# Token tiles of the output projection in another order, its moving operands split in parts, and finer rings for the product by w_out

## The chip, the cores and the metric

The kernel runs on one core of a Trainium2 chip. The metric is the time of one execution on the device in microseconds (us), as a median of runs; lower is better. Beside the runs there is one execution that the hardware profiler recorded, and all rows of the profile come from it. The engines are named as in the profile: PE is TensorE (matmuls, with PEld its weight loads), DVE is VectorE, ACT is ScalarE, POOL is GpSimd, and SP is the engine that issues the DMA transfers here. L12 is line 12 of the kernel before.

## The reference

The kernel computes a trunk of two encoder layers over 1024 tokens of width 1024, all in float32:

```python
for i in range(DEPTH):                      # 2 layers
    g = norm_g[i]
    h = rms_norm(x, g[0])
    if i % 2 == 0:
        m = neighborhood_attention(h, ...)  # 16 heads, 8 x 16 windows on a 16 x 64 grid
    else:
        m = diff_attention(h, ...)          # 8 heads, dense, T5 bias
    # both mixers end with  o @ w_o  (1024 x 1024), the output projection
    x = x + rms_norm(m, g[1])
    f = conv_glu_ffn(rms_norm(x, g[2]), w_in, conv_w, conv_b, w_out)
    x = x + rms_norm(f, g[3])
    gate = jax.nn.sigmoid(rms_norm(x, g[4]) @ ple_w_gate[i])
    x = x + gate * (p[i] @ ple_w_proj[i])

def conv_glu_ffn(h, w_in, conv_w, conv_b, w_out):
    gate, val = split(h @ w_in, 2)          # w_in 1024 x 5632, halves of 2816
    gate = conv3(gate, conv_w) + conv_b     # along the tokens, per channel
    return (gelu_tanh(gate) * val) @ w_out  # w_out 2816 x 1024
```

## The kernel before, in words

**Matmuls and splits.** A product of two float32 matrices is made of three matmuls on split operands (`mm3`, L107 to L109, and `times_steps`, L635): each operand is cut into a high part, rounded by ACT (L85), and a low part, which DVE makes as the operand minus the high part (L86). A split (`split`, L81) is therefore one ACT and one DVE instruction, the second waiting for the first. A matmul takes a stationary block of 128 x 128 and a moving block of 128 x 512. Transposes (L137) are matmuls with an identity matrix, eight for a token tile of 128 tokens.

**Order.** Only PE's order is the order of the program text (`manual_schedule`). DVE, ACT, POOL and the SP queue are ordered by a planner, which runs the program through a timeline of its own, takes what is ready and prefers what stands earlier in the text. Each engine then works strictly in that order. Tiles come from pools with a fixed number of buffers per tag; a tile in a new pool waits for the tiles of the old pool that lay at the same addresses, in the order in which the tags were first asked for.

**The output projection (`mix_out`, L660).** It runs over eight token tiles t. For each, PE makes 48 matmuls with w_o (tile 0 has most of its own earlier). Then follows a chain of one column and one row operation after another: squares on ACT with sums (L734), the sums added on DVE (L735), scaled and EPS added (L120), the power -1/2 on POOL (L121), the normed product on DVE (L739), the residual added (L742), its store, squares again (L115), L120, L121, and the normed h on DVE (L129). The transposes of tile t - 1 stand behind the matmuls of tile t, and `put` (L693) turns their result into the moving operands of the product by w_in. That product is made by Winograd's form of Strassen's method, with seven products of half size for each block of 128 channels: its moving operands are the quadrants B11, B21, B22 and the sums T1 to T4, with B11 and B21 from tiles 0 to 3, and the others needing tile t and tile t - 4 (t from 4 to 7). For t of 4 to 7 `put` makes T1 and T2 on DVE and ACT (L705 to L711) and leaves in b12 and b21, by three sums on POOL (L714, L716), what becomes T3 and T4. After the last tile, T3, B22 and T4 are split whole, 2048 columns each (L752 to L754).

**Begun blocks (`gate_begun`, L785).** After the last tile's matmuls and the transposes of the last tile but one, PE makes two products each on B11 and B21 for the blocks f = 0 and 1 (48 matmuls), while the last tile's h is made; then the last transposes; then `gated` (L801) goes on with the product on T2. The weights' sums S for Strassen's method (L847 to L850) are made on POOL, in the first half of a spare tile; the second half holds p1 of f = 0 and 1 and later Z, the sums of the activations (L900 to L903), which go to memory as the spills S1 to S4, beside the spills A11, A12 and A22.

**The product by w_out (`mixed`, L910).** Seven products (A11, A12, S1, S4, S2, S3, A22), again Strassen's, of 11 K tiles each; a K tile is 12 matmuls. They run in chunks of two K tiles (the last has one): a spill is loaded and split as stationary blocks, a quadrant of w_out, or a difference of two that `over` makes in place on DVE (L950), is split as the moving operand. The splits go to two rings of two slots, a slot holding a chunk. The quadrants lie in six pages of 16 KB per partition, four from the pool r2, two from r1, as rings are; one of these lies under the spare tile and can be loaded when the last spill of Z has been read.

**After it (`embed`, L986).** `residual` (L997) normalises tile t of the result and adds x1; `turn` (L1007) transposes it; then come the gate's matmuls (L635, `g`). `embed` runs the product by w_out as a generator: it takes it up to the sums of S3, emits residual 0 and 1, and goes through A22, with tile 0 turned after the fourth of eleven K tiles. The other tiles are turned ahead of their gate matmuls.

## Time and profile before

| what | value |
|---|---|
| runs | 2834.53, 2834.66, 2828.19 us; median 2834.53 |
| profiled execution, own time | 2829.02 us |
| its span in the profile | 2827.2 us, 36045 instructions |
| mean granted clock of PE | 0.985 of full speed |
| PE busy | 2715.1 us (96%), 13312 matmuls |
| DVE, ACT, POOL busy | 1961.5, 1320.9, 559.1 us |
| output projection, tiles 1 to 7, layers 0 and 1 | from 490.0 to 575.5 us, and to 2051.7 us |
| product by w_in | from there to about 1024 and 2498 us |
| product by w_out | to 1250.5 us in layer 0 |

Rows of a timeline give start, length, engine, line, operation, output and inputs with their shape, and in brackets how long the engine stood idle before it and what released it. Rows of waits give who waited for whom, and then us in total, times, and the longest. Rows of groups end with the count, the busy time, the mean in ns, and the idle time before them. The letter before an arrow is the written tile, by the program's names without their numbers: r stands for pages of both pools r1 and r2, b for a bank of PSUM.

### The profile page before, as it was taken

Reading aid. Unit: us, or ns where it says so; the run is one execution under the profiler, and the core shown is the slowest. Engines: PE = TensorE matmul, PEld = TensorE weight load, DVE = VectorE, ACT = ScalarE, POOL = GpSimd, SP = SyncE. Lnnn points to the kernel's source line nnn. Section 1 sums busy time; section 2 is a strip of 40 time slices with the busy share of each in tenths; the row PEclk is TensorE's granted clock in tenths of the full one; section 3 lists DMA queues with packets and bytes.
Section 4 is the critical chain, followed back from the end, with each engine's and each line's share of the span. In section 5 each row is a group of like instructions: output and inputs, shape, how many; then the busy total and the mean of one; then the engine's idle time right before and its main releaser. Section 6 shows DMA issues by size and latency. Waiting matters only on the chain.

```text
span 2827.2 us, 36045 instructions
## 1 busy us (share of the span) xinstructions
PE 2715.1 (96%) x13312; PEld 2261.6 (80%) x13312; DVE 1961.5 (69%) x3223; ACT 1320.9 (47%) x2331; POOL 559.1 (20%) x513
## 2 busy tenths in 40 slices
PE   7999999979999999999999999999979999999999
PEld 5788887758888878778888888887858888878777
DVE  5677776678777775566677777776677676666564
ACT  4555556444444434354455555565444444434352
POOL 2121220153433401001000000000254334301000
PEclk9999999989999999999999999999989999999999
DMA  6512215512232272243211111115313323372343
GB/s 186 160 52 66 66 45 184 146 58 105 107 109 99 99 287 89 86 155 110 96 45 45 45 45 45 37 52 180 126 60 105 112 98 107 109 261 93 104 147 104
DMA packets 129185, 298.44 MB, mean 106 GB/s; under 512 B 11721, under 2 KB 37705, under 8 KB 129009
## 3 DMA queue, kind: packets, MB, share of 16 engines
q1 hardware_dynamic: 129008, 296.15, 31.7%
q8 instruction: 104, 1.70, 0.2%
q14 instruction: 73, 0.59, 0.1%
HBM read 221.69 MB, written 86.61 MB: 109 GB/s over the span
## 4 chain that ended last, share of the span: by engine, by line
PE 84%; DVE 6%; DMA 5%; issue 2%; ACT 1%; POOL 1%; SPq 0%; DVEq 0%; ACTq 0%; POOLq 0%
PE b L108 19%; PE b L107 19%; PE b L109 19%; PE g L635 6%; PE b L554 4%; PE m L635 4%; DVE r L86 2%; PE s L516 2%; PE s L517 2%; PE b L540 2%; PE b L137 2%; DMA r<-in_ffn_w_out 2%; PE av L427 2%; PE b L411 1%; DMA x<-in_x 1%
## 5 line engine op out<-in xcount | busy, mean ns | idle before, releaser
L107 PE MATMUL b<-r,ws 128*128 128x512 f32 (+1 forms) x1312 | 542.2, 413 | 3.5 <-ACT ws L85 3.5
L109 PE MATMUL b<-r,ws 128*128 128x512 f32 (+1 forms) x1312 | 514.1, 392 | 0.5 <-DVE ws L86 0.5
L108 PE MATMUL b<-r,ws 128*128 128x512 f32 (+1 forms) x1312 | 513.1, 391 | 1.3 <-DVE r L86 1.1
L107 PE MATMUL b<-r,wa 128*128 128x512 f32 x704 | 276.5, 393 | 29.6 <-ACT wa L85 27.8
L121 POOL TENSOR_TENSOR ss<-ss,mhalf 128x1 f32<-128x1 f32 x136 | 86.9, 640 | 1098.1 <-DVE ss L120 1095.7
L109 PEld LDWEIGHTS b<-r,ws 128*128 128x128 f32 x1312 | 249.1, 190 | 53.5 <-DVE ws L86 1.0
L369 ACT ACTIVATE E<-E,mn 128x1024 f32<-128x1024 f32 (+2 forms) x256 | 221.6, 866 | 147.6 <-DVE mn L365 147.0
L107 PEld LDWEIGHTS b<-r,ws 128*128 128x128 f32 x1312 | 250.2, 191 | 48.5 <-ACT ws L85 4.0
L108 PE MATMUL b<-r,r 128*128 128x512 f32 x680 | 268.9, 395 | 14.8 <-DVE r L86 14.8
L108 PEld LDWEIGHTS b<-r,ws 128*128 128x128 f32 x1312 | 250.8, 191 | 38.4 <-DVE r L86 2.6
L109 PE MATMUL b<-r,wa 128*128 128x512 f32 x704 | 275.9, 392 | 4.0 <-DVE wa L86 4.0
L107 PE MATMUL b<-r,r 128*128 128x512 f32 x680 | 270.1, 397 | 6.6 <-ACT r L85 6.2
L108 PE MATMUL b<-r,wa 128*128 128x512 f32 x704 | 275.6, 392 | 0.0
L109 PE MATMUL b<-r,r 128*128 128x512 f32 x680 | 266.8, 392 | 0.0
L85 ACT ACTIVATE r<-raw 128x1024 fp32r<-128x1024 f32 x108 | 108.2, 1003 | 242.6 <-PE b L108 211.8
L86 DVE TENSOR_TENSOR r<-raw,r 128x1024 fp32r<-128x1024 f32 x108 | 126.6, 1173 | 123.5 <-ACT r L85 123.3
L86 DVE TENSOR_TENSOR ws<-raw,ws 128x512 fp32r<-128x512 f32 (+3 forms) x168 | 156.5, 939 | 73.7 <-ACT ws L85 72.0
L85 ACT ACTIVATE ws<-raw 128x512 fp32r<-128x512 f32 (+3 forms) x168 | 124.2, 748 | 145.4 <-PE b L109 57.0
L635 PE MATMUL g<-r,ws 128*128 128x512 f32 x768 | 181.3, 396 | 6.3 <-DVE facc L983 6.3
L107 PEld LDWEIGHTS b<-r,wa 128*128 128x128 f32 x704 | 133.4, 189 | 58.5 <-ACT wa L85 28.2
L365 DVE CUSTOM_DVE_ANT_0 E<-s,T 128x1024 f32<-128x1024 f32 x128 | 156.5, 1223 | 33.8 <-PE s L517 32.8
L635 PEld LDWEIGHTS g<-r,ws 128*128 128x128 f32 x768 | 145.3, 191 | 36.6 <-DVE facc L983 6.8
(173 smaller groups left out, 5360.8 us busy)
## 6 DMA issues: line engine op xcount, KB each, us to landing
raw<-in_w_in SPq DMA_DIRECT2D x88, 512.0 KB, 3.5
raw<-in_qkv SPq DMA_DIRECT2D x48, 512.0 KB, 5.6
spillS<-r SPq DMA_DIRECT2D x88, 256.0 KB, 2.7
r<-in_ffn_w_out SPq DMA_DIRECT2D x40, 512.0 KB, 10.0
raw<-spillS SPq DMA_DIRECT2D x40, 512.0 KB, 3.6
spillA<-cv SPq DMA_DIRECT2D x66, 256.0 KB, 2.6
raw<-spillA SPq DMA_DIRECT2D x30, 512.0 KB, 3.9
x<-x SPq DMA_DIRECT2D x24, 512.0 KB, 3.7
```

What stands on the lines that cost most here:

```text
L85: nc.scalar.activation(hi, src, AF.Copy)
L86: nc.vector.tensor_tensor(out=lo, in0=src, in1=hi.bitcast(F32), op=ALU.subtract)
L107: mm(out, sta[0], mov[0], start=first, stop=False, skip_group_check=onto)
L108: mm(out, sta[0], mov[1], start=False, stop=False, skip_group_check=onto)
L109: mm(out, sta[1], mov[0], start=False, stop=last, skip_group_check=onto)
L121: nc.gpsimd.tensor_tensor(out=ss, in0=ss, in1=self.mhalf, op=ALU.pow)
L137: self.nc.tensor.transpose(t[:, k * P : k * P + P], h[:, c : c + P], self.ident)
L365: nc.vector.tensor_tensor_reduce(out=e, in0=s, in1=bias, scale=1.0, scalar=3e38, op0=ALU.add, op1=ALU.min, accum_out=mn)
L369: nc.scalar.activation(e, e, AF.Exp, bias=mn, scale=-1.0, accum_out=sm)
L427: nc.tensor.matmul(out, V[:, kb, m], a[:, at * P : (at + w) * P], start=i + z == 0, stop=i == len(steps) - 1 and z == 1)
L554: nc.tensor.matmul(o, wT[:, k], V[:, k], start=k == 0, stop=k == KT - 1)
L635: mm(out[half], a, b[:, w], start=first and k + z == 0, stop=last and k == n - 1 and z == 2)
```

## The change

The diff does four things.

1. *The projection.* The tiles are taken in the order 0, 4, 1, 5, 2, 3, 6, 7. The pages of x, then g1 and g2, then h are asked for before b12, b21 and b22. The three sums of `put` for tiles 4 to 7 go from POOL to DVE. `gate_begun` becomes a generator: its first part, the load and the splits of the weights of f = 0, stands before the last tile's matmuls, the rest where all of it stood. The late splits are cut in two: the columns of the first three of their four tiles, for T3, B22 and T4, and after these the columns of the last tile.
2. *Weights' sums.* For f = 0 and 1 the four sums S are made on DVE, for later f on POOL as before.
3. *The product by w_out.* The rings hold four slots of one K tile each, in the same space; each K tile is split by itself (512 columns for 1024). The sixth page is the first half of the spare tile. The difference that S3 takes is made during S2, and the one that A22 takes during S3. The generator gives way before S3, so that residual 0 and 1 stand ahead of S3, and then once a chunk; tiles 0 and 1 are turned after the third and fifth of A22's six chunks.
4. *Columns.* The squares are scaled by 1/32 on ACT; in the projection the two half sums and EPS are added by one instruction with two scalars.

```diff
@@ rstd, rstd_of @@
-        nc.scalar.activation(junk, src, AF.Square, scale=scale, accum_out=ss)
-        nc.vector.tensor_scalar(out=ss, in0=ss, scalar1=1.0 / width, scalar2=EPS, op0=ALU.mult, op1=ALU.add)
+        self.nc.scalar.activation(junk, src, AF.Square, scale=D**-0.5, accum_out=ss)
+        self.nc.vector.tensor_single_scalar(out=ss, in_=ss, scalar=EPS, op=ALU.add)
...
@@ mix_out @@
+            W, last = self.W, self.opage
+            order = (0, 4, 1, 5, 2, 3, 6, 7)
+            ready = [self.page(x, "x"), self.page(x, "x")]
             g1 = self.bcast(x, "g1", self.i["norm_g"][layer, 1], bufs=1)
             g2 = self.bcast(x, "g2", self.i["norm_g"][layer, 2], bufs=1)
+            hs = [self.page(x, "h"), self.page(x, "h")]
             b12, b21, b22 = (self.page(x, k, (P, 4, 512), bufs=1) for k in ("B12", "B21", "B22"))
...
-                        on = nc.gpsimd.tensor_tensor
-                        on(out=of(b21, t), in0=of(b21, t), in1=of(b12, t), op=sub)
+                        tt(out=of(b21, t), in0=of(b21, t), in1=of(b12, t), op=sub)
                         for a in both("B11", t):
-                            on(out=of(b12, t), in0=of(b12, t), in1=a.bitcast(F32), op=sub)
+                            tt(out=of(b12, t), in0=of(b12, t), in1=a.bitcast(F32), op=sub)
...
-            for t in range(NT):
+            for n, t in enumerate(order):
...
-                nc.vector.tensor_tensor(out=ss[0], in0=ss[0], in1=ss[1], op=ALU.add)
-                r = self.rstd_of(ss[0], D)
+                nc.vector.tensor_scalar(out=r, in0=r, scalar1=ss[1], scalar2=EPS, op0=ALU.add, op1=ALU.add)
+                self.root(r)
...
-                if t > 0:
-                    self.transposed(hs[t - 1], put(t - 1))
-            begin(layer, X)
+                if n > 0:
+                    self.transposed(hs[n - 1], put(order[n - 1]))
+                if n == NT - 2:
+                    begin = begin(layer, X)
+                    next(begin)
+            next(begin)
             self.transposed(hs[-1], put(NT - 1))
-            for k, a in (("T3", b12), ("B22", b22), ("T4", b21)):
+            late = (("T3", b12), ("B22", b22), ("T4", b21))
...
+            for k, a in late:
                 X[k] = self.page(self.r1, "r1", (P, 2, 4, 512), F32R)
-                self.split(a, X[k][:, 0], X[k][:, 1])
+                self.split(first_three(a), first_three(X[k][:, 0]), first_three(X[k][:, 1]))
+            for k, a in late:
+                self.split(of(a, NT - 1), *both(k, NT - 1))
...
@@ gated @@
-                tt = nc.gpsimd.tensor_tensor
+                tt = (nc.gpsimd if f > 1 else nc.vector).tensor_tensor
...
@@ mixed @@
-        rings = [self.page(self.r1, "r1", (P, 2, 2, 2, 512), F32R) for _ in range(2)]
-        pages += [self.page(self.r1, "r1", (P, 2, 4, 512)) for _ in range(2)]
+        rings = [self.page(self.r1, "r1", (P, 4, 2, 512), F32R) for _ in range(2)]
+        pages.append(self.page(self.r1, "r1", (P, 2, 4, 512)))
+        pages.append(self.spare[:, :4].rearrange("p (c q) w -> p c q w", c=1))
...
-                self.split(raw[:, :c], sta[:, 0, :c], sta[:, 1, :c])
-                self.split(mov(n), b[:, 0, :c], b[:, 1, :c])
+                b = mov(n)
                 for i in range(c):
+                    at = self.turns % 4
+                    self.turns += 1
+                    (sh, sl), (bh, bl) = ((r[:, at, 0], r[:, at, 1]) for r in rings)
+                    self.split(raw[:, i], sh, sl)
+                    self.split(b[:, i], bh, bl)
...
+        def beside(n, *a):
+            over(n, *a)
+            return n
...
-        whole(one, "S2", lambda n: over(n, 0, 3, 0), True)
+        whole(one, "S2", lambda n: over(beside(n, 1, 3, 1), 0, 3, 0), True)
...
-        whole(one, "S3", lambda n: over(n, 1, 3, 1), False)
+        yield
+        whole(one, "S3", lambda n: quadrant(beside(n, 2, 2, 0), 1), False)
...
-        yield
-        yield from product(one, "A22", lambda n: over(n, 2, 2, 0), False)
+        yield from product(one, "A22", lambda n: quadrant(n, 2), False)
...
@@ embed @@
         for n, _ in enumerate(product):
-            if n == 3:
-                turn(0)
+            if n in (2, 4):
+                turn(n // 2 - 1)
...
-                if t + 1 < NT:
+                if 1 < t + 1 < NT:
                     turn(t + 1)
```

More of the change, by code (lines that the diff above doesn't have):

```diff
@@ L555, in da_values @@
         os = self.page(x, "os", (P, P))
-        r = self.rstd(o, os, P, scale=r0)
+        r = self.col("ss")
+        nc.scalar.activation(os, o, AF.Square, scale=r0, accum_out=r)
+        nc.vector.tensor_scalar(out=r, in0=r, scalar1=1.0 / P, scalar2=EPS, op0=ALU.mult, op1=ALU.add)
+        self.root(r)
         nc.vector.tensor_scalar(out=os, in0=o, scalar1=r0, scalar2=r, op0=ALU.mult, op1=ALU.mult)
@@ L711, in of_group @@
                         self.split(of(b12, t), *both("T2", t))
-                        on = nc.gpsimd.tensor_tensor
-                        on(out=of(b21, t), in0=of(b21, t), in1=of(b12, t), op=sub)
+                        tt(out=of(b21, t), in0=of(b21, t), in1=of(b12, t), op=sub)
                         for a in both("B11", t):
-                            on(out=of(b12, t), in0=of(b12, t), in1=a.bitcast(F32), op=sub)
+                            tt(out=of(b12, t), in0=of(b12, t), in1=a.bitcast(F32), op=sub)
                 return of_group
-            ready = [load(0), load(1)]
-            hs = []
-            for t in range(NT):
+            ready = [load(t, ready[n]) for n, t in enumerate(order[:2])]
+            for n, t in enumerate(order):
                 hi, lo, xi = ready.pop(0)
                 part = [(hi[:, k], lo[:, k]) for k in range(KT)]
-                h = self.page(x, "h")
+                h = hs[n] if n < 2 else self.page(x, "h")
+                if n >= 2:
+                    hs.append(h)
                 if t == 0:
@@ L733, in mix_out @@
                 for half in range(2):
-                    nc.scalar.activation(h[:, half * 512 : half * 512 + 512], m[half], AF.Square, accum_out=ss[half])
-                nc.vector.tensor_tensor(out=ss[0], in0=ss[0], in1=ss[1], op=ALU.add)
-                r = self.rstd_of(ss[0], D)
+                    w = slice(half * 512, half * 512 + 512)
+                    nc.scalar.activation(h[:, w], m[half], AF.Square, scale=D**-0.5, accum_out=ss[half])
+                r = ss[0]
+                nc.vector.tensor_scalar(out=r, in0=r, scalar1=ss[1], scalar2=EPS, op0=ALU.add, op1=ALU.add)
+                self.root(r)
                 for half in range(2):
@@ L785, in gate_begun @@
     def gate_begun(self, layer, X):
-        A = [self.weights_of(layer, 0), None]
+        A = [self.weights_of(layer, 0)]
         o = [[self.operand(A[0]["A11"]), self.operand(A[0]["A12"])]]
-        A[1] = self.weights_of(layer, 1)
+        yield
+        A.append(self.weights_of(layer, 1))
         o.append([self.operand(A[1]["A11"]), self.operand(A[1]["A12"])])
@@ L799, in gate_begun @@
             self.product(self.begun[f][1], o[f][1], X["B21"], False)
+        yield
     def gated(self, layer, X, spill):
@@ L1001, in residual @@
             h[t] = self.page(x, "h", bufs=2)
-            r = self.rstd(f, h[t], D)
+            r = self.rstd(f, h[t])
             nc.vector.scalar_tensor_tensor(out=f, in0=f, scalar=r, in1=g3, op0=ALU.mult, op1=ALU.mult)
```

35 lines of the change are left out of this document (16 added, 19 removed).

## The prediction, made blind

> **What bounds the kernel now.** I read the page first, then the waits of TensorE, then busy time in 20 us stretches, then the timelines of the engines where those stretches are thin.
>
> ```profile
> span 2827.2 us, 36045 instructions
> PE 2715.1 (96%) x13312; PEld 2261.6 (80%) x13312; DVE 1961.5 (69%) x3223; ACT 1320.9 (47%) x2331; POOL 559.1 (20%) x513
> ```
>
> TensorE (PE) is busy 96% of the span, and the change leaves its instructions as they are. What it can win is PE's idle time (2827.2 - 2715.1 = 112 us) and what a lowered clock costs after idle time. The waits of PE over the span:
>
> ```profile
> PE b L107 <- ACT wa L85: 27.8, 2, 13.9
> PE b L108 <- DVE r L86: 15.9, 19, 1.4
> PE b L137 <- DVE h L129: 13.1, 7, 3.1
> PE g L635 <- DVE facc L983: 6.3, 2, 3.3
> PE b L107 <- ACT r L85: 6.2, 3, 3.3
> ```
>
> The first row's two waits of 13.9 us stand once in each layer, at the end of the output projection; the third row's seven are 1.6, 1.7, 3.1 and 1.5 in layer 0 and 1.8, 3.1 and 0.3 in layer 1, at transposes of the projection. Stretches (length, PE busy and its matmuls, weight loads, DVE, ACT, POOL, granted clock, DMA share, GB/s): first a full one, then the thin ones.
>
> ```profile
> 680.00:700.00 20.00, 20.00 (x90) 16.57 (x89) 17.01 (x24) 8.43 (x13) 7.97 (x5) 1.00 0.33 118
> ...
> 580.00:600.00 20.00, 13.28 (x56) 10.46 (x55) 16.10 (x21) 7.00 (x12) 11.24 (x9) 0.84 0.18 53
> 600.00:620.00 20.00, 9.35 (x28) 6.99 (x29) 13.09 (x11) 11.31 (x14) 7.03 (x5) 0.58 0.16 49
> 1040.00:1060.00 20.00, 15.92 (x63) 12.16 (x62) 16.27 (x17) 5.87 (x7) 0.00 (x0) 0.93 0.87 309
> 1060.00:1080.00 20.00, 20.00 (x81) 16.34 (x80) 7.17 (x6) 7.93 (x10) 0.00 (x0) 0.90 0.20 66
> 2520.00:2540.00 20.00, 16.58 (x65) 13.01 (x64) 11.26 (x12) 6.80 (x9) 0.00 (x0) 0.91 0.55 175
> ```
>
> A full stretch holds 90 matmuls, 20/90 = 0.222 us each; 600-620 holds 28. So the losses sit at the end of the projection (560-620, and from 2040 in layer 1) and where the product by w_out begins (1040-1080, 2500-2540).
>
> **End of the output projection, step by step.** PE in layer 0 (the first row an undisturbed tile), then the two rows of layer 1 that answer the second and fifth:
>
> ```profile
> 514.51 1.03 PE L137 MATMUL b<-ident,h 128*128 128x128 f32 x8
> 564.34 11.17 PE L635 MATMUL m<-r,ws 128*128 128x512 f32 x48
> 578.61 1.36 PE L137 MATMUL b<-ident,h 128*128 128x128 f32 x8 [3.10 <-DVE h L129]
> 593.70 1.07 PE L137 MATMUL b<-ident,h 128*128 128x128 f32 x8 [1.50 <-DVE h L129]
> 608.66 0.80 PE L107 MATMUL b<-r,wa 128*128 128x512 f32 x1 [13.89 <-ACT wa L85]
> 611.88 0.79 PE L109 MATMUL b<-r,wa 128*128 128x512 f32 x1 [1.99 <-DVE wa L86]
> ...
> 2040.50 11.16 PE L635 MATMUL m<-r,ws 128*128 128x512 f32 x48
> 2084.68 0.79 PE L107 MATMUL b<-r,wa 128*128 128x512 f32 x1 [13.88 <-ACT wa L85]
> ```
>
> The last tile's matmuls end at 564.34 + 11.17 = 575.5. Then come the transposes of the last tile but one, 48 matmuls on B11 and B21, the last transposes, and at 608.66 the first matmul on T2: 33.2 us after 575.5, of which 48 x 0.227 = 10.9 and two sets of transposes are work. In layer 1 it is 2084.68 - 2051.7 = 33.0. What holds it, on DVE, POOL and ACT:
>
> ```profile
> 523.01 1.28 DVE L129 SCALAR_TENSOR_TENSOR h<-x,ss,g 128x1024 f32<-128x1024 f32 x1 [0.73 <-POOL ss L121]
> 591.26 2.29 DVE L129 SCALAR_TENSOR_TENSOR h<-x,ss,g 128x1024 f32<-128x1024 f32 x1 [0.44 <-POOL ss L121]
> 594.38 0.69 DVE L705 TENSOR_TENSOR B<-b,r 128x512 f32<-128x512 f32 x1 [0.82 <-PE b L137]
> 598.60 1.22 DVE L86 TENSOR_TENSOR r<-B,r 128x512 fp32r<-128x512 f32 x1 [0.70 <-ACT r L85]
> 599.97 2.58 POOL L716 TENSOR_TENSOR B<-B,r 128x512 f32<-128x512 f32 x2 [0.69 <-DVE r L86]
> 602.58 5.51 ACT L85 ACTIVATE r<-B 128x2048 fp32r<-128x2048 f32 x3 [4.01 <-POOL B L716]
> 604.52 6.70 DVE L86 TENSOR_TENSOR r<-B,r 128x2048 fp32r<-128x2048 f32 x3 [4.70 <-ACT r L85]
> ```
>
> T2 is whole at 598.60 + 1.22 = 599.8, but the operand wa stands behind POOL's last sums (to 602.55) and the three splits of 2048 columns on ACT and DVE (to 608.1 and 611.2).
>
> The change takes that queue apart: three quarters of each late split (1536 columns) no longer need the last tile, the sums go from POOL to DVE, the first sums for the weights too, and the pages of x, g1, g2 and h come first in the pool, so that wa no longer lies over B12 and B21, which the late splits read last.
>
> What I expect of the step: 11.7 us of PE work after the last matmuls (transposes 0.8, products 10.9), then the last tile's h. Its chain took 524.29 - 514.51 = 9.8 us where nothing disturbed it (the h at 523.01, of the matmuls that ended as the transposes at 514.51 began), against 593.55 - 575.5 = 18 at the end. With put(6) on DVE in between I allow 13.0, so 1.3 us of wait. From h to the end of T2 it was 599.8 - 593.55 = 6.3 us; I keep 6.5. T2 starts 13.0 + 6.5 = 19.5 us after the last matmuls. Later waits in f = 0 and 1 were 2.0 and 1.9 in layer 0, 2.0 in layer 1; with DVE fuller I charge 3 and 2. **Gain: 33.2 + 3.9 - 19.5 - 3 = 14.6, and 33.0 + 2.0 - 19.5 - 2 = 13.5 us.** Bounds: from 0, if DVE keeps its order, to 20 a layer, if h and operands are never late.
>
> What DVE is given: L714 and L716 on POOL,
>
> ```profile
> L716 POOL TENSOR_TENSOR B<-B,r 128x512 f32<-128x512 f32 x8 | 11.4, 1428 | 1.5 <-DVE r L86 0.7 <-DVE ss L120 0.7
> L714 POOL TENSOR_TENSOR B<-B,B 128x512 f32<-128x512 f32 x4 | 6.9, 1730 | 5.8 <-DVE B L710 5.8
> L129 DVE SCALAR_TENSOR_TENSOR h<-x,ss,g 128x1024 f32<-128x1024 f32 x8 | 13.3, 1658 | 8.8 <-POOL ss L121 8.8
> ```
>
> 12 sums, and 8 for the weights of f = 0 and 1: 20 x 0.62 (the pitch of the 0.69 us at 594.38 and its neighbours) = 12.4 us a layer. It is given back part: L129 takes 1.28 us with POOL at rest and 1658 ns in the mean here, 8 x 0.38 = 3.0 us, and other DVE rows beside POOL's sums are as much longer (the 1.22 at 598.60 for 0.69). I take DVE as 5 to 9 us fuller, which is in the 13.0 and the 3 above. The two other tiles with sums, 4 and 5, now come at steps 1 and 3, where PE has 11.2 us of matmuls over DVE; before, L129 was late by 1.74 us after the first such tile (layer 0) and 1.75 (layer 1). I expect 0.7 left of each: gain 1.0 a layer, bounds -3 to +1.7. The first wait of layer 0 (1.6 us, for x) is from x landing late under the old order of pages; I take 1.0 of it.
>
> [...] The trace: after a wait of 3.27 us at 1057.41 the stretches read 0.93 and 0.90, and 1060-1080 holds 81 matmuls for 90, 9 x 0.222 = 2 us lost, and a third of the 1040-1060 loss with it. [...]
>
> **The product by w_out.**
>
> ```profile
> 1046.64 4.00 DMA spillS<-r
> 1050.71 1.90 SPq L927 DMA_DIRECT2D r<-in_ffn_w_out  x4
> 1057.41 0.79 PE L107 MATMUL b<-r,r 128*128 128x512 f32 x1 [3.27 <-ACT r L85]
> 1062.34 0.43 PE b L108
> PE b L108 <- DVE r L86: 4.9, 5, 1.4
> L86 DVE TENSOR_TENSOR r<-raw,r 128x1024 fp32r<-128x1024 f32 x16 | 19.5, 1220 | 23.3 <-ACT r L85 23.3
> L86 DVE TENSOR_TENSOR r<-raw,r 128x512 fp32r<-128x512 f32 x4 | 2.8, 688 | 0.0
> L85 ACT ACTIVATE r<-raw 128x1024 fp32r<-128x1024 f32 x16 | 16.9, 1058 | 51.9 <-PE b L108 51.2 <-ACT r L85 0.8
> L85 ACT ACTIVATE r<-raw 128x512 fp32r<-128x512 f32 x4 | 2.5, 630 | 1.6 <-PE b L108 1.6
> ```
>
> The last page of w_out was issued at 1050.71, once the last store of the sums (1046.64 to 1050.64) had left the page under it; the new page is the half of the spare tile that those stores do not use, free as soon as the last weights are split. That removes 3.27 us and 15 matmuls at 0.43 for 0.227, 3.0 us (the row at 1062.34 is one of them). In layer 1 the like wait is 2.4 us, and 2520-2540 holds 65 matmuls for 90: 25 x 0.222 = 5.6 us in all. Together 11.9; SP's queue and the transfers are full here, so I take 10. Bounds 0 (the pieces land as late anyway) to 11.9.
>
> The waits of L108 of up to 1.4 us stand where one product follows another: the last chunk is one K tile, 12 x 0.227 = 2.7 us of PE, and the next chunk's two splits of 1024 on ACT and two on DVE take 1.06 + 1.04 + 1.22 + 1.22. The row gives them for 1062 to 1225, and it reads the same for 2540 to 2700: 4.9 us a layer. With four slots of one K tile three tiles, 8.2 us, lie ahead. I take 4 a layer, bounds 0 to 4.9. The price of halves is in the rows: 2 x 630 for 1058 on ACT, 2 x 688 for 1220 on DVE, that is 2 x (0.63 + 0.69) = 2.64 us a K tile spread over two engines, under 2.7 us of PE; nothing on the path. The sums for S2 and S3 now both stand in S2: 2 x 1.22 for two K tiles beside 4 x 0.69 of splits on DVE, 5.2 of 5.4 us if none is taken ahead. In the ring's lead I cost that at nothing; without that cover, up to 5 us a layer.
>
> Turning tile 1 earlier takes its transposes from between the product and the gate. There PE waits 3.3 us for the last sums (L983), and has that much less to do meanwhile (1.0 us, eight transposes): I charge 0.5 a layer. The two-scalar add in place of two DVE columns of 0.15 us is in the noise.
>
> **Sum:** 14.6 + 13.5 + 2 x 1.0 + 1.0 = 31.1 for the projection, 10 + 8 = 18 for the product, minus 1: 48 us. The profiled execution took 2829.0 us (span 2827.2); the median of the runs is 2834.5, 5.5 above it, two of three at 2834.6 and one at 2828.2. 2829.0 - 48 = 2781, and 2 us for standing between those: **2783 us**.
>
> **Rivals.**
> - *Operand splits still behind.* If T2's operand keeps standing behind the late splits (now 1536 columns: 0.75 of the 8.6 us from 602.58 to 611.2, and 3 x 0.62 for the last tile's parts), T2 starts 8.4 us later than I say in both layers: 2783 + 17 = 2800. For it: ACT and DVE work in order, and the parts are ready before the last h. Against: the operand's pages come free sooner.
> - *w_out lands late anyway.* The DMA share is 0.87 in 1040-1060 with the wait in it. Then only the boundaries are won: 2783 + 10 = 2793.
> - *All of it closes.* T2 ready at 16 us in both layers (7 more), no later waits (5), the full 4.9 twice and 11.9 (3.7): 2783 - 16 = 2767.
> - *Slower: DVE has no room.* In 580-600 DVE is busy 16.1 of 20 us. Where DVE's queue holds the 12.4 us of added sums ahead of L129, PE waits for each in full: 24.8 us in two layers, plus four waits over 3 us at tiles 4 and 5 with 1.4 us of clock each, 5.6, and none of the 31 won; with the product's 18 that is 2829 + 30.4 - 18 = 2841. It decides against the change once the added waits pass 18 us. Against it: POOL's own sums take longer (1730 and 1428 ns for 690) and hold DVE up meanwhile.
> - *It does not do what it says.* The order on ACT, DVE and SP is the planner's; if it had hoisted this work already, all stays within 8 us: 2829.
>
> **Chances.** Forecast 0.43; operands behind 0.16; w_out late 0.14; all closes 0.14; no room 0.07; no effect 0.06. A measurement here tells 0.3%, 8.5 us, from no change. Faster is the first four, 0.87; same 0.06; slower 0.07. The range 2760 to 2815 holds those four with the bounds of the terms.
>
> **What would show it.** Right: the first matmul on T2 about 19 us after the last tile's (33 before), its wait at 5 to 7 us for 13.9; no L714 to L716 on POOL, and L129 near 1.3 us; the last w_out issue before 1035; L108's waits on DVE in the product below 5 us in all for 15.9; the stretch at the product's start near 85 matmuls. Wrong: transposes waiting over 2 us at tiles 4 and 5, DVE above 19 of 20 us in the last stretches of the projection, or PE waiting for raw spills in the product.

## The result: the time that was forecast, and not from where it was forecast

The changed kernel takes 2786.9 us in the median of four runs (2783.7 to 2788.9), the kernel before 2833.7 us (2828.2 to 2834.7): ratio 0.9838, 95% interval 0.9821 to 0.9855. The medians differ by 46.8 us. The profiled executions differ by less, 40.1 us by their spans: that of before (2829.0 us) was near the quickest of its runs, that of the changed kernel (2788.9 us) the longest of its four. The parts below are of these 40.1. Lines are from here on those of the changed kernel: h is made at L127 (L129 before), the last sums at L1008 (L983 before), and the splits stay at L85 and L86. The kernel of a run that adds lines has each of them one or a few further on, as its rows show.

The page and TensorE's waits over the whole span:

```profile
span 2787.1 us, 36499 instructions
...
PE 2706.9 (97%) x13312; PEld 2260.9 (81%) x13312; DVE 1983.3 (71%) x3393; ACT 1341.0 (48%) x2477; POOL 495.0 (18%) x473
```

```profile
PE b L107 <- ACT wa L85: 27.2, 2, 13.6
...
PE g L637 <- DVE facc L1008: 8.5, 2, 4.4
...
PE b L135 <- DVE h L127: 2.1, 1, 2.1
PE b L108 <- DVE r L86: 0.5, 2, 0.3
```

The waits of the transposes for h went from 13.1 us in seven to 2.1 in one, those for DVE's splits at L108, of which 14.2 of 15.9 us stood in the product by w_out, to 0.5, and the late last page no longer shows. But the largest row stayed: PE still stands 13.6 us before T2 in each layer, and the wait for the last sums before the gate grew from 6.3 to 8.5 us.

The stretches that were thin before, in the same view. The product by w_out starts earlier now, at 1015.1 us for 1024.3 in layer 0 and at 2467.3 for 2497.4 in layer 1. So the row for layer 1 is the stretch that lies as far behind this start as 2520 to 2540 did before.

```profile
580.00:600.00 20.00, 9.94 (x48) 8.09 (x47) 18.75 (x25) 10.67 (x16) 1.46 (x1) 0.86 0.10 27
600.00:620.00 20.00, 16.44 (x63) 13.28 (x64) 15.54 (x24) 10.27 (x18) 6.92 (x5) 0.80 0.20 57
1040.00:1060.00 20.00, 18.96 (x84) 15.38 (x83) 13.88 (x22) 9.57 (x18) 0.00 (x0) 1.00 0.51 164
1060.00:1080.00 20.00, 20.00 (x90) 16.57 (x89) 12.03 (x18) 10.42 (x19) 0.00 (x0) 1.00 0.33 106
2490.00:2510.00 20.00, 20.00 (x89) 16.54 (x89) 15.31 (x23) 10.10 (x19) 0.00 (x0) 1.00 0.45 146
```

The start of the product by w_out is full (84 and 90 matmuls for 63 and 81, clock 1.00 for 0.93 and 0.90; in layer 1 89 for 65). The end of the projection is not, and there DVE is busy 18.75 of 20 us. The rows of PE's timeline by which the terms are read:

```profile
504.76 1.09 PE L135 MATMUL b<-ident,h 128*128 128x128 f32 x8 [2.07 <-DVE h L127]
...
566.14 11.15 PE L637 MATMUL m<-r,ws 128*128 128x512 f32 x48
603.56 0.80 PE L107 MATMUL b<-r,wa 128*128 128x512 f32 x1 [13.62 <-ACT wa L85]
...
1234.46 13.60 PE L637 MATMUL g<-r,ws 128*128 128x512 f32 x48 [4.12 <-DVE facc L1008]
...
2018.96 11.15 PE L637 MATMUL m<-r,ws 128*128 128x512 f32 x48
2056.38 0.79 PE L107 MATMUL b<-r,wa 128*128 128x512 f32 x1 [13.62 <-ACT wa L85]
```

The last tile's matmuls end at 566.14 + 11.15 = 577.3, and T2's first matmul follows at 603.56: a lag of 26.3 us, where it was 33.2 and the forecast was 19.5. In layer 1 it is 2056.38 - 2030.1 = 26.3, where it was 33.0. So each layer gained 6.9 and 6.7 us there, half of what was forecast. The wait for h inside the 33 us is gone; the wait for the operand is as long as it was.

What happens in these 26 us, on ACT and then on DVE:

```profile
589.98 0.60 ACT L713 ACTIVATE B<-b 128x512 f32<-128x512 f32 x1 [3.96 <-PE b L135]
590.47 5.25 ACT L85 ACTIVATE r<-B 128x1536 fp32r<-128x1536 f32 x5
599.04 1.35 ACT L85 ACTIVATE r<-B 128x512 fp32r<-128x512 f32 x2 [3.31 <-DVE B L714]
602.36 0.63 ACT L85 ACTIVATE r<-B 128x512 fp32r<-128x512 f32 x1 [1.97 <-DVE B L719]
602.89 1.66 ACT L85 ACTIVATE wa<-r 128x512 fp32r<-128x512 f32 x3
...
586.76 1.29 DVE L127 SCALAR_TENSOR_TENSOR h<-x,ss,g 128x1024 f32<-128x1024 f32 x1 [0.44 <-POOL ss L119]
...
590.61 0.69 DVE L710 TENSOR_TENSOR B<-B,r 128x512 f32<-128x512 f32 x1
591.98 6.30 DVE L86 TENSOR_TENSOR r<-B,r 128x1536 fp32r<-128x1536 f32 x5 [0.68 <-ACT r L85]
598.31 0.69 DVE L714 TENSOR_TENSOR B<-B,B 128x512 f32<-128x512 f32 x1
599.70 0.69 DVE L86 TENSOR_TENSOR r<-B,r 128x512 fp32r<-128x512 f32 x1
```

The last tile's h is ready at 586.76 + 1.29 = 588.05, which is 10.8 us after the last matmuls. Its B12 is ready on DVE at 591.3 (L710). The next step of T2 is L714, and it comes at 598.31: between them DVE makes five splits, 6.30 us, among them the three late parts of 1536 columns that the change made ready early. The planner put them into the gap. T2's own split so ends at 599.70 + 0.69 = 600.39. ACT does the same at 590.47, and wa, T2's other operand (the weights' half of its matmuls), stands on ACT behind the last late part (602.36) and is made from 602.89 on; PE starts when its first split is done.

To say where time went I use three segments for each layer on PE's timeline: the lag (from the end of the last tile's matmuls to the first matmul on T2), from T2 to the first matmul of the product by w_out, and from there to the gate's first. Each ratio is to the kernel before as it ran beside that run, with medians from 2831.2 to 2836.3 us, so the ratios tell more than the medians; runs 1 to 4, 5 to 8 and 9 to 11 ran side by side.

| kernel | lag, layers 0 and 1 | T2 to w_out | w_out to gate | median, us | ratio to before, 95% |
|---|---|---|---|---|---|
| before | 33.2, 33.0 | 415.6, 412.7 | 230.4, 229.1 | 2833.7 | |
| changed | 26.3, 26.3 | 411.6, 410.9 | 219.3, 218.3 | 2786.9 | 0.9838 (0.9821 to 0.9855) |
| changed, again | 26.3, 26.3 | 411.7, 411.1 | 218.8, 218.5 | 2784.2 | 0.9826 (0.9812 to 0.9839) |
| 1 projection only | 26.3, 26.3 | 411.4, 410.4 | 230.6, 229.7 | 2811.0 | 0.9925 (0.9910 to 0.9940) |
| 2 product only | 33.6, 33.2 | 417.4, 414.7 | 218.1, 217.9 | 2813.8 | 0.9934 (0.9919 to 0.9949) |
| 3 sums on POOL | 30.3, 30.3 | 413.1, 411.6 | 219.1, 217.8 | 2799.5 | 0.9885 (0.9868 to 0.9901) |
| 4 tiles 0 to 7 | 27.9, 27.9 | 412.8, 411.5 | 218.0, 217.8 | 2791.1 | 0.9855 (0.9840 to 0.9870) |
| 5 late splits whole | 25.1, 25.1 | 415.2, 413.8 | 218.1, 218.3 | 2791.3 | 0.9857 (0.9842 to 0.9872) |
| 6 old sixth page | 26.3, 26.3 | 411.5, 410.4 | 225.6, 219.7 | 2794.0 | 0.9868 (0.9853 to 0.9883) |
| 7 old rings | 26.3, 26.3 | 411.7, 410.8 | 225.1, 224.9 | 2799.5 | 0.9887 (0.9873 to 0.9902) |
| 8 late splits behind T2 | 18.6, 18.6 | 415.6, 417.2 | 219.2, 218.0 | 2784.7 | 0.9833 (0.9817 to 0.9849) |
| 9 last adds first | 26.3, 26.3 | 411.7, 411.8 | 216.4, 214.8 | 2778.0 | 0.9806 (0.9793 to 0.9820) |
| 10 runs 8 and 9, and x first | 18.6, 18.6 | 416.8, 414.7 | 216.5, 214.7 | 2776.7 | 0.9797 (0.9783 to 0.9811) |
| 12 old order of pages | 26.3, 26.3 | 411.5, 410.6 | 219.5, 218.6 | 2787.3 | 0.9832 (0.9813 to 0.9851) |

The lag of the changed kernel and of the runs that leave it alone repeats within 0.1 us; the others repeat within about 1.5 us. The tiles of the projection before the last took from 82.9 to 88.1 us in layer 0, where they wait for transfers (DVE at the first tile of the changed kernel 1.91 us for g1 and 2.71 for x). In layer 1 they took 84.1, 84.8 and 83.5 us in the three kernels with the sums on POOL (before, runs 2 and 3) and 81.7 to 83.2 in all others. So a segment tells smaller things than the medians do. By them the 40.1 us are: lag 6.9 + 6.7, T2 to w_out 4.1 + 1.8, w_out to gate 11.1 + 10.8, the tiles of the projection before the last -0.1 + 1.2, and -2.3 for all other stretches.

### The profile page after: what moved, and what is told of

Same layout as the page of the kernel before. It is cut to its first block, busy times and chain, and to the rows that moved or that the text cites. A ratio compares the mean times of both kernels' runs of the same rounds, so it can differ in the third digit from the quotient of the medians.

```text
span 2787.1 us, 36499 instructions
## 1 busy us (share of the span) xinstructions
PE 2706.9 (97%) x13312; PEld 2260.9 (81%) x13312; DVE 1983.3 (71%) x3393; ACT 1341.0 (48%) x2477; POOL 495.0 (18%) x473
## 4 chain that ended last, share of the span: by engine, by line
PE 89%; DMA 5%; DVE 3%; ACT 2%; issue 1%; SPq 0%; POOL 0%; ACTq 0%; DVEq 0%; POOLq 0%
PE b L107 21%; PE b L109 20%; PE b L108 20%; PE g L637 6%; PE m L637 5%; PE b L553 4%; PE s L515 2%; PE s L516 2%; PE b L539 2%; PE b L135 2%; PE av L426 2%; DVE r L86 1%; PE b L410 1%; DMA x<-in_x 1%; DMA raw<-in_qkv 1%; DMA raw<-in_ple_w_gate 1%
## 5 line engine op out<-in xcount | busy, mean ns | idle before, releaser
L108 PE MATMUL b<-r,ws 128*128 128x512 f32 (+1 forms) x1312 | 512.1, 390 | 0.6 <-DVE r L86 0.5
L119 POOL TENSOR_TENSOR ss<-ss,mhalf 128x1 f32<-128x1 f32 x136 | 87.5, 644 | 1141.0 <-DVE ss L557 566.0
L108 PEld LDWEIGHTS b<-r,ws 128*128 128x128 f32 x1312 | 250.0, 191 | 37.6 <-DVE r L86 1.9
L108 PE MATMUL b<-r,wa 128*128 128x512 f32 x704 | 275.8, 392 | 0.0
L108 PE MATMUL b<-r,r 128*128 128x512 f32 x680 | 265.4, 390 | 0.0
L86 DVE TENSOR_TENSOR r<-raw,r 128x512 fp32r<-128x512 f32 (+1 forms) x178 | 140.8, 795 | 111.8 <-ACT r L85 111.5
L85 ACT ACTIVATE r<-raw 128x512 fp32r<-128x512 f32 (+1 forms) x178 | 121.4, 687 | 205.2 <-PE b L108 166.2
L86 DVE TENSOR_TENSOR ws<-raw,ws 128x512 fp32r<-128x512 f32 (+3 forms) x168 | 155.3, 932 | 65.3 <-ACT ws L85 63.8
L85 ACT ACTIVATE ws<-raw 128x512 fp32r<-128x512 f32 (+3 forms) x168 | 124.3, 748 | 143.3 <-PE b L109 57.0
```

Of the source, the lines that this page charges most:

```text
L85: nc.scalar.activation(hi, src, AF.Copy)
L86: nc.vector.tensor_tensor(out=lo, in0=src, in1=hi.bitcast(F32), op=ALU.subtract)
L108: mm(out, sta[0], mov[1], start=False, stop=False, skip_group_check=onto)
L119: self.nc.gpsimd.tensor_tensor(out=ss, in0=ss, in1=self.mhalf, op=ALU.pow)
```

## The experiments

The theory after the first comparison: the projection gave 20 us since POOL's sums no longer hold the h chain up, and less than forecast since the late parts and wa now stand in front of T2; the product gave 22. The rivals are the sizes of the prediction, and that one part of the change alone made each gain. Each run undoes or adds one thing; where it is two at once, the text says so. No run leaves computation out.

**1 and 2: each half alone.** The first keeps `mixed` and `embed` of before in the changed file; the second puts the changed ones in the file before.

```diff
  run 1: the changed kernel with
-    def mixed(...), def embed(...)      # as changed
+    def mixed(...), def embed(...)      # as before
  run 2: the kernel before with
-    def mixed(...), def embed(...)      # as before
+    def mixed(...), def embed(...)      # as changed
```

> The output projection and the sums of the weights as changed (tile order, late splits in parts, sums on DVE), with the product by w_out and the pages as before. Theory from the two traces: the projection's part is worth 20 to 21 us of the 40 (6.9 and 6.8 at its two ends, the rest in what follows T2), so about 2813. Theory of the prediction's sizes: 31, so about 2803. If the parts need each other (the stores of the sums under the last page of w_out come earlier only when the projection does), it is worth less than 17 alone.

> The projection as before, the product by w_out as changed (six pages with the last in the spare tile, four slots of one K tile, splits of 512, the turned tiles earlier). Theory from the traces: 20 to 22 us, about 2812. Theory of the prediction's sizes: 17, about 2817. Theory that w_out lands late anyway: 10, about 2824.

Measured: 20.2 and 17.3 us under the median of before beside them (2831.2). The first agrees with the trace's 20 to 21 and not with 31. The median of the second would fit the 17 of the prediction, but its profile shows the product's segments shortened by 12.3 and 11.2 us, more than in the whole change. What its median lacks lies elsewhere: its transposes wait longer for h (16.6 us in all for 13.1), and its segment from T2 to w_out is 1.8 and 2.0 us longer. Waits of PE in run 1 and then in run 2:

```profile
PE b L108 <- DVE r L86: 15.0, 18, 1.4
```

```profile
PE b L137 <- DVE h L129: 16.6, 7, 3.1
```

Each half removes its own rows and leaves those of the other. The two ratios multiplied give 0.9860, just above the interval of the whole change (0.9821 to 0.9855); with 0.0015 of uncertainty in each factor I read no interaction from that.

**3: the sums on POOL again.**

```diff
-                        tt(out=of(b21, t), in0=of(b21, t), in1=of(b12, t), op=sub)
+                        on = nc.gpsimd.tensor_tensor
+                        on(out=of(b21, t), in0=of(b21, t), in1=of(b12, t), op=sub)
                         for a in both("B11", t):
-                            tt(out=of(b12, t), in0=of(b12, t), in1=a.bitcast(F32), op=sub)
+                            on(out=of(b12, t), in0=of(b12, t), in1=a.bitcast(F32), op=sub)
...
-                tt = (nc.gpsimd if f > 1 else nc.vector).tensor_tensor
+                tt = nc.gpsimd.tensor_tensor
```

> The changed kernel with put's sums and the sums for the weights of f = 0 and 1 on POOL again, nothing else altered. Theory that POOL's sums hold the h chain up: the waits of the transposes for h come back (3 us and more at the second and fourth tile and near the end), T2 starts 30 us or more after the last tile's matmuls for 26.3, and it is 8 to 14 us slower than the changed kernel, about 2798. Theory that the gain came from the order and the parts alone: within 3 us of the changed kernel. Theory that DVE lacks room for the sums: faster than it.

Measured: 2799.5 us, ratio 0.9885 against 0.9838, some 13 us slower than the changed kernel by the ratios and 10.5 by the spans of the profiles. This is the largest single part of the projection's gain. The lag is 4.0 us longer in each layer, and from T2 to w_out come 1.5 and 0.8. The groups of instructions of run 3 over the whole span, and those of the changed kernel:

```profile
L127 DVE SCALAR_TENSOR_TENSOR h<-x,ss,g 128x1024 f32<-128x1024 f32 x16 | 28.7, 1796 | 13.6 <-POOL ss L119 13.6
L720 POOL TENSOR_TENSOR B<-B,r 128x512 f32<-128x512 f32 x16 | 26.7, 1670 | 2.0 <-DVE r L86 1.4
```

```profile
L127 DVE SCALAR_TENSOR_TENSOR h<-x,ss,g 128x1024 f32<-128x1024 f32 x16 | 20.5, 1284 | 7.4 <-POOL ss L119 7.4
L719 DVE TENSOR_TENSOR B<-B,r 128x512 f32<-128x512 f32 x16 | 11.0, 689 | 0.3
```

The instruction that makes h takes 1796 ns in the mean with the sums on POOL and 1284 without them, and what it waits for, POOL's column L119, comes later too: it idles 13.6 us ahead of these sixteen for 7.4. POOL takes 1670 ns for a sum that DVE does in 689. The h at 590.20 of run 3 takes 2.31 us, and two of POOL's sums (L720) run beside it, from 590.14 to 593.65; why DVE is slower there was not shown. Of the 3 us waits for h only a part came back (the longest is 1.7 us); that the order of the tiles, which spreads the sums, covers the rest was not tried apart.

**4: the tiles in the order 0 to 7.**

```diff
-            order = (0, 4, 1, 5, 2, 3, 6, 7)
+            order = tuple(range(NT))
```

> The changed kernel with the tiles in the order 0 to 7. Tiles 4 to 7 carry the sums, and now come together at the end. Theory that spreading them is what the order does: T2 starts 2 to 6 us later after the last tile's matmuls than 26.3, with waits for h, 4 to 12 us slower, about 2795. Theory that with the sums on DVE the order no longer matters: within 3 us.

Measured: ratio 0.9855 (0.9840 to 0.9870), which overlaps that of the changed kernel, and its profiled span was shorter (2784.7 us). The lag grows by 1.7 us a layer, just under the 2 to 6 expected. The tiles before take 1.6 and 1.2 us less than in the first profile of the changed kernel, but 81.7 us in layer 1 is also what run 11, the changed kernel again, shows. So with the sums on DVE the order is worth 1.7 us a layer by the lag, and the times of the whole kernel are too coarse to confirm it. (The lag is read from these rows of run 4: 561.98 + 11.14 = 573.1 to 601.06.)

```profile
561.98 11.14 PE L637 MATMUL m<-r,ws 128*128 128x512 f32 x48
...
601.06 0.80 PE L107 MATMUL b<-r,wa 128*128 128x512 f32 x1 [14.45 <-ACT wa L85]
```

**5: the late splits whole.**

```diff
             for k, a in late:
                 X[k] = self.page(self.r1, "r1", (P, 2, 4, 512), F32R)
-                self.split(first_three(a), first_three(X[k][:, 0]), first_three(X[k][:, 1]))
-            for k, a in late:
-                self.split(of(a, NT - 1), *both(k, NT - 1))
+                self.split(a, X[k][:, 0], X[k][:, 1])
```

> The changed kernel with the late splits undivided again (2048 columns on ACT and DVE, not 1536 for the first three tiles and 512 for the last). Theory that the order of work on ACT and DVE holds T2, and the parts only fill that order ahead of T2's own split: T2 26 us after the last tile's matmuls as in the changed kernel, within 2 us either way, or earlier, since nothing is ready to stand ahead of T2's split; then the later operands are late instead. Theory that the halving gained the 6.9 us: T2 at 31 to 33 us, 10 us slower over both layers.

Measured: T2 comes 1.2 us sooner, not later, and what follows is later by 3.6 and 3.0 us; the ratio is 0.9857 (0.9842 to 0.9872), 4 us above the changed kernel and barely to be told from it. So the cut does not gain the 6.9 us. It shifts work: with whole splits nothing is ready early, T2's split is free of them, and the operands behind T2 are late instead, as the second row of run 5 shows, the wait of 2.0 us that stood in the same place before. DVE's split of T2 ends at 596.98 there, and PE still waits until 604.55: ACT makes wa only behind the three late splits. Here wa alone holds the product.

```profile
604.55 0.80 PE L107 MATMUL b<-r,wa 128*128 128x512 f32 x1 [12.41 <-ACT wa L85]
607.76 0.80 PE L109 MATMUL b<-r,wa 128*128 128x512 f32 x1 [1.99 <-DVE wa L86]
...
598.47 5.51 ACT L85 ACTIVATE r<-B 128x2048 fp32r<-128x2048 f32 x3 [2.21 <-DVE B L719]
603.88 1.66 ACT L85 ACTIVATE wa<-r 128x512 fp32r<-128x512 f32 x3
```

**12: the old order of pages.** The prediction held that T2's operand comes free sooner since wa no longer lies over B12 and B21.

```diff
-            ready = [self.page(x, "x"), self.page(x, "x")]
             g1 = self.bcast(x, "g1", self.i["norm_g"][layer, 1], bufs=1)
             g2 = self.bcast(x, "g2", self.i["norm_g"][layer, 2], bufs=1)
-            hs = [self.page(x, "h"), self.page(x, "h")]
             b12, b21, b22 = (self.page(x, k, (P, 4, 512), bufs=1) for k in ("B12", "B21", "B22"))
+            ready = [self.page(x, "x"), self.page(x, "x")]
+            hs = [self.page(x, "h"), self.page(x, "h")]
```

> The changed kernel with the pages of its pool in the order of before: g1, g2, B12, B21 and B22 ahead of those of x and h, so that the operands wa of the next stage lie again over B12 and B21, which the late splits read last. Theory that the place of wa matters to T2: wa of f = 0 waits for the last late split (DVE at 603.6 in the changed kernel) and T2 starts 28 to 30 us after the last tile's matmuls for 26.3, 4 to 6 us slower in all. Theory that wa waits only for its turn on ACT: T2 within 0.5 us of 26.3, and the same time within 3 us.

Measured: nothing moves. The lag is 26.27 us in both layers, the same wait of 13.62 us, and the ratio 0.9832 (0.9813 to 0.9851).

```profile
601.02 0.79 PE L107 MATMUL b<-r,wa 128*128 128x512 f32 x1 [13.62 <-ACT wa L85]
```

wa waits for its turn on ACT, not for its place. In the kernel before, too, ACT made T2's wa from 608.00 on, while DVE read the late operands until 611.2.

**8: the late splits behind T2's.** The late splits are queued on ACT and DVE behind the split of the last tile's T2, and the sums and first two operands of f = 0 are made in `gate_begun`, in the pages ws. These are two things at once.

```diff
-                        self.split(of(b12, t), *both("T2", t))
+                        self.t2 = self.split(of(b12, t), *both("T2", t))   # the two instructions
...
+            with self.tc.issue_after(self.t2[0]), self.tc.issue_after(self.t2[1]):
                 for k, a in late:
...
         # end of gate_begun
+        S = self.spare[:, :4].rearrange("p s (k n) -> p s k n", k=4)
+        self.sums(self.nc.vector.tensor_tensor, S, self.begun[0][0])
+        self.early = self.operand(S[:, 1]), self.operand(S[:, 0])   # s2, s1 of f = 0
```

> The changed kernel with the late splits queued on ACT and DVE behind the split of the last tile's T2, and the weights' sums and first two operands of f = 0 made earlier, in pages of their own. Theory that T2 waits only because the late parts and wa stand in its way: T2 18 to 20 us after the last tile's matmuls for 26.3; of those 6 to 8 us a layer up to half is lost again at the later operands, 2773 to 2780. Theory that the splits as a whole are what T2 waits for, whatever their order: T2's gain is lost in full at the next products, 2785 to 2790.

Measured: the lag is 18.6 us in both layers, the wait 5.9. PE's timeline, and the rows of DVE behind T2:

```profile
568.32 11.15 PE L638 MATMUL m<-r,ws 128*128 128x512 f32 x48
598.03 0.80 PE L108 MATMUL b<-r,ws 128*128 128x512 f32 x1 [5.91 <-ACT r L85]
...
2047.56 0.79 PE L108 MATMUL b<-r,ws 128*128 128x512 f32 x1 [5.91 <-ACT r L85]
...
599.39 1.76 DVE L86 TENSOR_TENSOR r<-B,r 128x1536 fp32r<-128x1536 f32 x1
...
601.66 5.22 DVE L86 TENSOR_TENSOR r<-B,r 128x1536 fp32r<-128x1536 f32 x5
606.81 0.69 DVE L896 TENSOR_TENSOR u<-b,r 128x512 f32<-128x512 f32 x1
```

So it was these splits and wa that held T2, and the 19.5 us with a wait of 5 to 7 were to be had. But of the 7.7 us a layer 4.0 and 6.3 are lost again from T2 to w_out: the late parts now fill DVE until 606.8, the sum u (L896) stands behind them, and short waits follow (0.96, 0.75, 0.55 and 1.13 us in layer 0). The ratio is 0.9833 against 0.9838, which is no difference that can be told. Both theories were half right: order decides T2, and DVE's total work decides what is left of it.

**6 and 7: the product's two parts.** Run 6 takes the sixth page from r1 again, under the stores of the sums; run 7 takes two slots of two K tiles and splits of 1024 columns again.

```diff
  run 6
-        pages.append(self.page(self.r1, "r1", (P, 2, 4, 512)))
-        pages.append(self.spare[:, :4].rearrange("p (c q) w -> p c q w", c=1))
+        pages += [self.page(self.r1, "r1", (P, 2, 4, 512)) for _ in range(2)]
  run 7
-        rings = [self.page(self.r1, "r1", (P, 4, 2, 512), F32R) for _ in range(2)]
+        rings = [self.page(self.r1, "r1", (P, 2, 2, 2, 512), F32R) for _ in range(2)]
...
-                for i in range(c):
-                    at = self.turns % 4
-                    self.split(raw[:, i], sh, sl)
-                    self.split(b[:, i], bh, bl)
+                at = self.turns % 2
+                self.split(raw[:, :c], sta[:, 0, :c], sta[:, 1, :c])
+                self.split(mov(n), b[:, 0, :c], b[:, 1, :c])
```

> The changed kernel with the sixth page of w_out under the stores of the sums again, rings of four slots kept. Theory that the page's place made the wait of 3.27 and 2.39 us at the product's start: a wait of 2 to 3 us of the first operand and matmuls at half clock after it come back, 4 to 6 us a layer, about 2796. Theory that the deeper ring covers it: within 2 us of the changed kernel.

> The changed kernel with rings of two slots of two K tiles and splits of 1024 again, the new page kept. Theory that the chunk boundaries made the waits on DVE: 4.9 us a layer come back, about 2797, with the first operand in time. Theory that the page alone did it: within 2 us of the changed kernel.

Measured for the page: 2794.0 us, ratio 0.9868, 7 and 10 us above the two medians of the changed kernel. The segment to the gate is 6.3 us longer in layer 0 and 1.3 in layer 1. PE's timeline of run 6:

```profile
1044.49 0.79 PE L107 MATMUL b<-r,r 128*128 128x512 f32 x1 [4.32 <-ACT r L85]
...
2499.59 0.50 PE L107 MATMUL b<-r,r 128*128 128x512 f32 x1 [0.77 <-ACT r L85]
```

In layer 0 the theory of the place holds, in layer 1 that of the deeper ring: with it the late page costs 0.77 us for the 2.4 of before. Measured for the rings: 2799.5 us, ratio 0.9887, 13 and 15 us above these medians, the segments 5.8 and 6.5 us longer, and one row of PE's waits is back:

```profile
PE b L108 <- DVE r L86: 14.0, 18, 1.4
```

So the rings (slots and splits together) are the larger part of the product, 12.3 us of the 21.9, the page 7.6. The remaining 2.0 fit the layer 1 wait, which either part covers alone; but the differences made earlier and the earlier turns were not tried apart.

**9: the last adds first.** The wait that grew stands before the gate: DVE adds the last product's four banks (L1008), and the gate's first matmuls take over these banks. In the changed kernel the adds at 1229.78, 1231.92 and 1233.12 stand between splits of turned tile 1 (L86) and of the gate's weights (L89):

```profile
1230.72 1.28 DVE L89 SCALAR_TENSOR_TENSOR r<-raw,g,r 128x1024 fp32r<-128x1024 f32 x1 [0.26 <-ACT r L88]
1231.92 0.69 DVE L1008 TENSOR_TENSOR facc<-b,facc 128x512 f32<-128x512 f32 x1
1232.52 0.68 DVE L86 TENSOR_TENSOR ws<-b,ws 128x512 fp32r<-128x512 f32 x1
```

Run 9 turns tiles 0 and 1 a chunk earlier and queues the second half of the weights' splits behind the last add.

```diff
-            if n in (2, 4):
-                turn(n // 2 - 1)
+            if n in (1, 3):
+                turn(n // 2)
...
+            # resident(..., behind=self.last_add): for kt >= 4
+            with self.tc.issue_after(behind):
                 self.load_split(...)
```

> The changed kernel with the start of the gate in another order: tiles 0 and 1 are turned one chunk earlier (in chunks 1 and 3 of the last product), and the splits of the second half of the gate's weights are queued on DVE and ACT behind the last add L1008. Theory that the last adds are late because DVE does splits of turned tiles and of weights between them: PE's wait for g falls from 4.1 to 1 to 2 us and its first 48 matmuls no longer run at 13.5 us for 10.9, 4 to 6 us a layer, about 2777. Theory that the adds cannot come sooner, or that the weights are then late: the wait is renamed, within 3 us of the changed kernel.

Measured: 2778.0 us, beside 2784.2 for the changed kernel on the same chip. DVE and PE of run 9:

```profile
1224.92 2.73 DVE L1009 TENSOR_TENSOR facc<-b,facc 128x512 f32<-128x512 f32 x4 [0.37 <-PE b L109]
1236.23 1.23 DVE L1030 TENSOR_TENSOR facc<-facc,raw 128x1024 f32<-128x1024 f32 x1 [1.50 <-DMA raw<-x]
...
1227.70 11.18 PE L638 MATMUL g<-r,ws 128*128 128x512 f32 x48 [0.78 <-DVE facc L1009]
1240.53 1.06 PE L135 MATMUL b<-ident,h 128*128 128x128 f32 x8 [1.65 <-DVE ss L115]
```

The four adds run in one go, the wait is 0.78 us for 4.12, and the first 48 matmuls take 11.18 us for 13.60. A wait of 4.1 us had thus cost 4.1 + 2.4. A new wait of 1.65 us behind them takes a part back: the next tile's norm waits for the sum with x1 (L1030), and DVE stood idle 1.50 us before that sum until the transfer of x1 came. Why this transfer is late was not tried. The theory of the interleaved splits holds. The gain of 6.2 us is 3 a layer, less than the 4 to 6 expected; the new wait explains a part of that.

**10 and 11: all together, and the changed kernel again.** Run 10 joins runs 8 and 9 and issues x of the first two tiles ahead of g1 and g2; run 11 is the changed kernel beside them.

```diff
  run 10: runs 8 and 9, and
+            ready = [load(t, ready[n]) for n, t in enumerate(order[:2])]
             g1 = self.bcast(x, "g1", self.i["norm_g"][layer, 1], bufs=1)
             g2 = self.bcast(x, "g2", self.i["norm_g"][layer, 2], bufs=1)
...
-            ready = [load(t, ready[n]) for n, t in enumerate(order[:2])]
```

> The changed kernel with the late splits behind T2's, the gate's start as in the run with the adds first, and the loads of x for the first two tiles of the projection issued on SP ahead of those of g1 and g2. Theory that the three are separate places of loss: their sum, about 2 us from the late splits, 8 to 12 from the gate's start, 1 to 3 from x in layer 0 (the first transposes' wait of 2.07 us at 504.76 falls below 1), about 2773. Theory that the gains are taken back at the next wait: within 3 us of the changed kernel.

> The changed kernel itself, on the chip of the two runs before, so that they are compared with it directly: 2784 to 2791, and the same segments as its first profile within 2 us but for the first tiles of layer 0.

Measured: 2776.7 and 2784.2 us. Run 10 is faster than both kernels (ratio to before 0.9797, interval 0.9783 to 0.9811; the changed kernel beside it 0.9826, 0.9812 to 0.9839), by 7.6 us against the changed one, between the 2773 us of the sum and the 3 us of the second theory. Nearly all of that is run 9's; the late splits add what they did alone, nothing that can be told. x first gained nothing. SP's queue and DVE at the first tile of run 10:

```profile
487.80 1.23 SPq L680 DMA_DIRECT2D x<-in_x  x2
489.07 1.06 SPq L141 DMA_DIRECT2D g<-in_norm_g  x2
...
497.49 1.41 DVE L748 SCALAR_TENSOR_TENSOR h<-b,ss,g 128x512 f32<-128x512 f32 x2 [5.48 <-DMA g<-in_norm_g]
```

x is in time, and the same tile now waits 5.48 us for g1 instead, where the changed kernel waited 1.91 for g1 and then 2.71 for x. The transfers are full there (a DMA share of 0.98 from 490 to 500 us in the changed kernel, 0.89 in run 10); the order says only which of the four comes late.

## Why the prediction was right in sum, and wrong in its parts

The forecast was 2783 us and the median 2786.9. The terms were 31.1 for the projection, 18 for the product, minus 1 for the gate. Measured on the segments: 20.6 and 21.9 with the gate in it. Two errors of opposite sign hid in the sum. That the median lies so near is in part luck: the terms were worked out from profiled executions, and between these 40.1 us came of the 48; the other 6.7 us are the scatter of the two profiled executions about their medians.

- *The wait for h: right.* The four waits at the end, and those at tiles 4 and 5, are gone; L127 takes 1284 ns, and the last h is ready 10.8 us after the last matmuls, where 13.0 were allowed. Run 3 shows why in part: with the sums on POOL L127 took 1796 ns, and stood 13.6 us in all behind POOL's column L119 for 7.4.
- *T2 at 19.5 us: wrong, and it is the step that failed.* "From h to the end of T2 it was 599.8 - 593.55 = 6.3 us; I keep 6.5" assumed that nothing new comes between, and that T2 is the last operand. From h to the end of T2 it is 600.39 - 588.05 = 12.3 us, since five splits of 6.30 us stand there on DVE, and wa comes 3.1 us later still (603.5), behind the last late part on ACT. That is the rival "Operand splits still behind", which gave 8.4 us a layer (its terms, 0.75 x 8.6 + 3 x 0.62, add to 8.3); measured are 6.8. Its mechanism held and the forecast's did not, though the total landed on the forecast. Run 8 gives the counterproof: with the late splits behind T2, the lag is 18.6 us and the wait 5.9.
- *wa and the pages: wrong.* "so that wa no longer lies over B12 and B21" changes nothing for T2 (run 12); wa waits for its turn on ACT.
- *What the 6.9 us are made of* is settled for a part: 4.0 come from the sums on DVE (run 3), 1.7 from the order (run 4), the cut of the splits gives -1.2 (run 5), the pages 0 (run 12). The remaining 2.4 were not isolated; they may lie in two of the parts together, or in the first part of `gate_begun`, which stands earlier and was not tried apart.
- *The later waits: charged too much.* 3 and 2 us were charged; measured is one of 0.9 us in layer 0 and none in layer 1, and the segment from T2 to w_out is 4.1 and 1.8 us shorter. That is the side on which the cut of the late splits pays (3.6 and 3.0 us, run 5). In run 8, where T2 did come at 18.6 us, the charge would have been too small: 4.0 and 6.3 us were lost.
- *x late in layer 0, gain 1.0: wrong.* The wait is 2.07 us for 1.60. The transfers are full there in either order (a DMA share of 0.98 from 490 to 500 us, and 0.89 in run 10).
- *Tiles 4 and 5, gain 1.0 a layer: right in layer 1* (1.2 us over all tiles before the last, and up to 2.4 in the runs with 81.7); in layer 0 the first tile lost as much again. It is due to the sums on DVE and not to the order: in layer 1 the stretch is long in the three kernels with the sums on POOL, and with the order 0 to 7 it is no longer (run 4).
- *Last page of w_out, 10: too large.* Run 6 says 7.6, of which 6.3 are layer 0; in layer 1 the deeper ring covers the page too.
- *Boundaries, 8: mis-sized.* Run 7 says 12.3. The prediction read 4.9 us a layer from 1062 to 1225 and left out the same waits at the product's start, 1.6 us in layer 0 and 2.8 in layer 1, which stand in its own row of 15.9. Its price for halves (nothing on the path) was right: 0.5 us of waits are left. So were 85 matmuls at the product's start (84) and the last issue of w_out before 1035 us, by SP's row of the changed kernel:

```profile
1018.94 4.65 SPq L948 DMA_DIRECT2D r<-in_ffn_w_out  x4
```

- *The gate, 0.5 a layer: mis-sized.* The wait grew by 0.8 and 1.4 us. What holds PE there are splits between the adds (run 9). What made the wait grow was not tried apart; it is 3.8 and 3.6 us in run 1 too, where the gate's start and the product are those of before.
- *The clock: near what the sum took for it.* The granted clock reads 0.53 from 1235 to 1240, behind the wait of 4.12 us, and the loss is 13.60 - 11.18 = 2.4 us; the sum had 3.0 for the wait of 3.27 us. Behind shorter waits clock was lost as well: behind 2.07 us 48 matmuls took 12.78 us for 11.15 (at 505.61), and behind 3.02 us, in the kernel before, 12.64 for 11.18, 1.5 us lost where the slower rival has 1.4 for each wait. Behind 2.33 us in run 10 they took 11.18 (at 2685.02): these rows do not tell the loss by the length of the wait alone.
- *The slower rival* (DVE has no room): DVE reaches 18.75 of 20 us in the stretch before T2, but no transpose waits for h there, and run 3, which takes the work off DVE, is slower. It falls.

## What to carry to other kernels

Work that the change made ready earlier was put by the planner into the first gap it fitted, and the gap was on the path: after cutting a late operand, look at what now stands between the two steps of the chain, and queue the pieces behind it by hand. Moving POOL's elementwise sums to DVE paid although DVE was the fuller engine, since POOL took 1670 ns for a sum that DVE makes in 689, and with these sums on POOL the instruction on DVE that makes h took 1796 ns in the mean for 1284. When waits for full queues are traded (x for g1, T2 for u), a segment between two fixed matmuls tells gain from renaming, where the length of one wait does not.

## What the runs showed of the hardware that was not expected

The shorter wait of run 8 did not save the clock. Behind the 13.62 us before T2 the first eleven matmuls came 4.76 us apart in all (603.56 to 608.32) where full speed gives 11 x 0.227 = 2.5; behind the 5.91 us of run 8 thirteen took 5.99 for 2.95. The loss is 2.3 us in the one and 3.0 in the other, and 2.4 behind the 4.12 us before the gate: these three waits differ by up to 9.5 us, and the losses behind them by up to 0.7. The shortest cost nothing of the kind: 48 matmuls took 11.18 us behind the 0.78 us of run 9, and 11.16 and 11.17 behind 1.60 and 1.74 us in the kernel before (at 503.51 and 564.34).
